# A gate row in four pieces of two column groups, second parts on VectorE, and pooling inputs loaded first, in a hybrid attention, Fourier and pooling layer

## The chip, the cores and the metric

The kernel runs on one core of a Trainium2 chip, as one launch. The metric is the device time of that launch in microseconds. The five engines of the core work from queues of their own, in order, and wait for each other by semaphores: PE is TensorE (matmuls, with their weight loads shown as PEld), DVE is VectorE, ACT is ScalarE, POOL is GpSimd, and SP is SyncE, which here issues all DMA transfers. SBUF is the on-chip memory, PSUM the eight banks into which matmuls accumulate, DRAM the memory outside.

## What is computed

One layer of a diffusion backbone, for 1024 sample tokens and 128 prompt tokens (1152 columns in all), with 1024 channels. The parts of the reference that matter here:

```python
h = _rmsnorm(x, norm_g) * (1 + scale) + shift          # shift, scale, gate = silu(cond) @ w_ada + b_ada
q, k, v, z_a, u_b, z_b, u_c, z_c, g_a, g_b, g_c = jnp.split(h @ w_in, SPLIT_POINTS, axis=-1)
y_a = attend(q, k, v)
y_b = _fourier(u_b, w_fnet)                            # real part of a 2-D DFT, then a linear map
y_c = _pool(u_c, w_pool, pool_scale)                   # windows 2, 4, 8, 16: mean minus self, then a linear map
merged = (sigmoid(g_a) * ((silu(z_a) * y_a) @ p_a)
        + sigmoid(g_b) * ((silu(z_b) * y_b) @ p_b)
        + sigmoid(g_c) * ((silu(z_c) * y_c) @ p_c))
return x + gate * (merged @ w_o), k, v
```

The residual gate is one row of 1024 numbers for each of the two conditionings (context and sample): `silu(cond)` times the last third of `w_ada`, plus its bias. Matmuls are made exact enough by splitting each operand into a high part and a remainder (first part and second part below) and adding three products.

## The kernel before

The program has these stages, one after the other: conditioning and h, the projections with attention (to 427 us), the pooling and Fourier branches (427 to 505 us), the branch projections `p_c`, `p_b`, `p_a` (505 to 636 us), the merge gates (to 884 us), and the output projection.

**Pooling and Fourier branches.** Here the order on each engine is set by the framework's scheduler, which starts from the order of the code. The gates z_c and z_b come in four row tiles of three chunks of 384 columns, 24 matmuls a chunk (`z_chunk`, tiles `zc`, `zb`); after each chunk ACT takes the sigmoid (line 992) and DVE multiplies (line 993). The same call prepares the weights of the next row tile: a matmul sums squares (`pw_m`), DVE, POOL and DVE again make a power of two from it (lines 94, 95, 96, 90; tile `wsc_m`), ACT makes the first part of the weights (line 112, `wh_m`), DVE the second (line 113, `wl_m`). The inputs of the branches, `u`, lie in DRAM and are loaded as `uc` (pooling, two tiles of 128 channels) and `ub` (Fourier, two tiles). For each pooling tile DVE adds shifted copies (`pool_sums`, tiles `s`) and takes the difference from u (`pool_diff`, line 1080); ACT rounds it (`dh`, line 1081), DVE makes the remainder (`dl`, line 1082). Three chunks of three matmuls follow (`pool_out`, tile `yc`), whose results ACT takes out of PSUM (line 1091); `yc` has two PSUM banks, so that the third chunk waits until the first is out. `gate_chunk` multiplies with z, rounds on ACT (line 998, `th`) and makes the second part on POOL (line 999, `tl`). The small tiles of the pooling and channel constants are `pwt`, `ped`, `wpb` and `cw`; `W` is the product of the last.

**Branch projections.** From here the order is written out by hand. `p_chunk(n, c)` is chunk c (384 columns) of row tile n: for n from 0 to 15, 6 matmuls, alternately for p_c (tile `ppc`) and p_b (`ppb`); for n from 16 to 23, 12 matmuls of p_a (`ppa`). There are two PSUM banks for each of the three chunks. ACT copies a chunk to SBUF (line 1278, `pec`, `peb`, six tiles), SP stores it to DRAM (line 1264). DVE splits the weights of row tile n+2 (lines 72 and 73, `oh_p`, `ol_p`) from a raw tile `or` that was loaded four row tiles earlier. Between the chunks of n below 12 stands the gating of branch a: SP loads `ya` and `za` for n+2 (lines 1365 and 1366), ACT takes the sigmoid of `za` (line 1374), DVE multiplies, ACT rounds, POOL makes the second part (line 1383); DVE and ACT also work on combinations of h (`combos`).

**The gate row** is spread over the same 16 row tiles: `add_wg(m)` multiplies the 32 columns of `sil` with one of eight weight tiles `wg` of 128 rows and 1024 columns (two buffers, line 1348 loads them), one matmul for each half of the row (tile `gr`, line 1355), in the group of 32 array columns that m picks (`tile_position`). It is called after row tiles 1, 3, 5 and so on to 15. The four groups of array columns are summed at the end (ACT copies `gro`, matmul `gb`, line 1417). The conditioning stage computes shift and scale in the same way (line 398, tile `pa`), two weight rows of neighbouring column groups at a time.

Of the kernel before, what the change touches and what calls it, by code (L numbers as in the profile page):

```python
# [20 lines left out]
P = 128  # L21
# [18 lines left out]
def mixer_layer(ctx: ExitStack, tc: tile.TileContext, xs, xp, smalls, qgrow, kgrow, bgate, wss, wgate, w1, w3, pw, wo,  # L40
# [154 lines left out]
    with tc.tile_pool(name="hp", bufs=1, side="right") as hp:  # L195
# [770 lines left out]
        with ExitStack() as bctx:  # L966
# [28 lines left out]
            def gate_chunk(zs, y, dh, dl, a):  # L995

                V.tensor_tensor(zs, zs, y[:, a], op=ALU.mult)
                S.copy(dh[:, a], zs)
                G.tensor_tensor(dl[:, a], zs, dh[:, a].bitcast(F32), op=ALU.subtract)

            t_tiles(bctx.enter_context(tc.tile_pool(name="tc", bufs=1, side="right", **TW)), (2, 3))
            with ExitStack() as cctx:
# [23 lines left out]

                pwt = bp.tile([P, 2], F32, name="pwt")
# [13 lines left out]
                us = []  # L1041
                for i, name in enumerate(("c0", "c1", "b0", "b1")):
                    u = bo.tile([P, UW], F32, tag="u", name=f"u{name}", bufs=4)
                    if i < 2:
                        G.memset(u[:, 0:8], 0.0)
                        G.memset(u[:, 1032:1048], 0.0)
                        G.memset(u[:, 1176:1184], 0.0)
                    nc.sync.dma_start(u[:, 8:1032], u_d[i][:, 0:NS])
                    nc.sync.dma_start(u[:, UOFF[1]:UOFF[1] + P], u_d[i][:, NS:NT])
                    us.append(u)  # L1050
                wph, wpl = two(bp, wpb, [P, 2, P], "wp", "wpb")

                def pool_sums(i):
# [6 lines left out]
                    if i == 0:  # L1060
                        e.tensor_copy(s4[0:64, 8:UW - 8], s2[0:64, 8:UW - 8])
# [6 lines left out]
                    e.tensor_copy(s16[0:64, 8:UW - 8], s8[0:64, 8:UW - 8])  # L1068
# [52 lines left out]

                zc1 = new_zs("c1")
# [5 lines left out]
                pool_out(1, *pool_diff(1, f1), zc1)  # L1128
# [60 lines left out]
                zbs = [new_zs("b0"), new_zs("b1")]  # L1189
                zq = []  # L1190

                def next_z():
                    i, c = divmod(len(zq), 3)
                    z_chunk(zbs[i], 10 + i, f"zb{i}", c)
                    zq.append(0)

                yb = [bo.tile([P, UW], F32, tag="u", name=f"yb{i}", bufs=4) for i in range(2)]
                f_ = fold("oe")
                next_z()
# [42 lines left out]
                for c in range(3):  # L1242
                    for i in range(2):
                        a = slice(c * CH, (c + 1) * CH)
                        gate_chunk(zbs[i][:, a], yb[i], th[i], tl[i], a)
# [96 lines left out]
            with tc.tile_pool(name="gp", bufs=1, **TW) as gp:  # L1342
# [9 lines left out]
                def add_wg(m):  # L1352
                    g = 32 * (m % 4)
                    for n in range(2):
# [39 lines left out]
                for n in range(16):  # L1394
# [12 lines left out]
                    if n % 2 == 1:  # L1407
                        add_wg(n // 2)
                        if n // 2 + 2 < 8:
                            load_wg(n // 2 + 2)  # L1410
# [361 lines left out]
```

## Time and profile before

| | us |
|---|---|
| median of three runs | 989.02 (987.64 to 989.61) |
| the profiled execution | 992.83 |
| its span, first to last instruction | 990.3 |
| branches, first zc matmul to first ppc matmul | 426.81 to 504.96 |
| projections p_c and p_b, first ppc matmul to the end of gb | 504.96 to 584.27 |

The profiled execution took 3.8 us longer than the median of the runs; times inside the trace are those of the profiled execution, in microseconds from the start of its span. A row of the timeline gives the start, the duration, the engine, the line, the operation, output and input tiles, and in square brackets how long the engine stood idle before it and what released it. A row of the windows gives a stretch and its length, then busy time (and the number of instructions) of PE, PEld, DVE, ACT and POOL, the granted clock of TensorE (1.00 is full speed), the busy share of the 16 DMA engines and their rate in GB/s.

### The profile page before, as it was taken

How to read it: one execution, taken by the hardware profiler on the slowest of the kernel's cores; microseconds unless marked ns; L12 is line 12 of the kernel's file. 1: busy time of each engine (PE TensorE's matmuls, PEld its weight loads, DVE VectorE, ACT ScalarE, POOL GpSimd, SP SyncE). 2: the span in 40 equal slices, each digit the busy share in tenths (PEclk: the TensorE clock that was granted, in tenths of full speed). 3: DMA queues.
4: the chain of work that ended last, by engine and by line, in shares of the span. 5: the costliest groups of instructions: out<-in, count | busy, mean ns of one | idle time of the engine just before them, and what ended most of it. 6: DMA issues, size and time to landing. Idle time of an engine off the chain costs nothing.

```text
span 990.3 us, 17726 instructions
## 1 busy us (share of the span) xinstructions
PE 922.5 (93%) x6554; PEld 677.0 (68%) x6554; DVE 658.8 (67%) x1443; ACT 489.7 (49%) x1017; POOL 208.4 (21%) x352
## 2 busy tenths in 40 slices
PE   4668899999989999998969999999999999999998
PEld 2324566666656666764757779988888888877886
DVE  2347767767767555549767868478989789765322
ACT  3354757757756646644535644545555454442100
POOL 0000765255254332002132200002021020200000
PEclk9568999999999999998988999999999999999999
DMA  7731351251241141250138965453444332228321
GB/s 300 276 107 37 79 152 44 59 170 34 57 131 33 48 149 55 104 188 0 59 104 291 318 237 197 152 176 96 152 126 122 129 105 79 67 71 297 117 75 53
DMA packets 75781, 125.02 MB, mean 126 GB/s; under 512 B 12031, under 2 KB 45227, under 8 KB 75695
## 3 DMA queue, kind: packets, MB, share of 16 engines
q1 hardware_dynamic: 75695, 123.89, 38.8%
q8 instruction: 51, 0.84, 0.3%
q14 instruction: 35, 0.29, 0.1%
HBM read 88.20 MB, written 29.11 MB: 118 GB/s over the span
## 4 chain that ended last, share of the span: by engine, by line
PE 77%; DVE 7%; ACT 5%; DMA 5%; issue 3%; POOL 2%; SPq 1%; ACTq 0%; DVEq 0%; POOLq 0%
PE p L166 3%; PE p L164 3%; PE p L165 3%; PE wo L164 3%; PE wo L166 3%; PE wo L165 3%; PE xc L164 3%; PE xb L164 3%; PE xb L166 3%; PE xc L166 3%; PE xb L165 3%; PE xc L165 3%; PE m L164 3%; PE m L166 3%; PE m L165 3%; PE xa L164 3%
## 5 line engine op out<-in xcount | busy, mean ns | idle before, releaser
L164 PE MATMUL p<-wh_q,hh 128*128 128x384 f16 x288 | 95.3, 331 | 1.9 <-ACT hh L457 1.9
L166 PE MATMUL p<-wh_q,hl 128*128 128x384 f16 x288 | 95.1, 330 | 1.1 <-DVE hl L458 1.1
L165 PE MATMUL p<-wl_q,hh 128*128 128x384 f16 x288 | 95.1, 330 | 0.0
L733 DVE CUSTOM_DVE_ANT_0 sn<-s,bias 128x512 f32<-128x512 f32 x64 | 44.0, 688 | 32.3 <-PE s L729 30.5
L164 PE MATMUL m<-hh,wh_m 128*128 128x384 f16 x192 | 62.6, 326 | 0.0
L166 PE MATMUL m<-hh,wl_m 128*128 128x384 f16 x192 | 62.6, 326 | 0.0
L165 PE MATMUL m<-hl,wh_m 128*128 128x384 f16 x192 | 62.6, 326 | 0.0
L164 PE MATMUL wo<-woh,mh 128*128 128x512 f32 x144 | 56.8, 394 | 1.2 <-ACT woh L1525 1.2
L165 PE MATMUL wo<-wol,mh 128*128 128x512 f32 x144 | 56.6, 393 | 0.0
L166 PE MATMUL wo<-woh,ml 128*128 128x512 f32 x144 | 56.4, 392 | 0.0
L754 ACT CAST pts<-pt 128x512 f16<-128x512 f32 (+1 forms) x72 | 39.7, 552 | 29.4 <-PE pt L752 28.0
L95 POOL TENSOR_SCALAR wsc_g<-wsc_g 128x1 f32<-128x1 f32 x12 | 2.6, 218 | 222.8 <-DVE wsc_g L94 222.8
L758 DVE TENSOR_TENSOR pts<-pt,pts 128x512 f16<-128x512 f32 (+1 forms) x72 | 46.2, 642 | 3.9 <-ACT pts L754 3.2
L744 ACT ACTIVATE sn<-sn,mn 128x512 f32<-128x512 f32 x64 | 46.2, 721 | 3.9 <-DVE mn L733 3.9
L1654 DVE TENSOR_TENSOR yo<-wo,gb 128x512 f32<-128x512 f32 x18 | 12.4, 691 | 50.1 <-PE wo L166 45.9
L777 DVE TENSOR_SCALAR yt<-po,ri,vf 128x64 f32<-128x64 f32 x72 | 24.7, 343 | 29.7 <-PE po L773 26.4
L166 PEld LDWEIGHTS <-hl 128*128 128x128 f16 x288 | 28.5, 99 | 21.0 <-DVE hl L458 1.8
L164 PEld LDWEIGHTS <-hh 128*128 128x128 f16 x288 | 28.8, 100 | 19.0 <-ACT hh L457 2.0
L166 PEld LDWEIGHTS <-wl_m 128*128 128x128 f16 x288 | 28.4, 99 | 19.3 <-issue 1.3
L164 PEld LDWEIGHTS <-wh_m 128*128 128x128 f16 x288 | 29.0, 101 | 17.3 <-issue 1.1
L290 POOL TENSOR_TENSOR rs<-rs,mhalf 128x4 f32<-128x4 f32 x36 | 40.0, 1110 | 3.0
L165 PEld LDWEIGHTS <-wh_m 128*128 128x128 f16 x288 | 28.4, 99 | 17.3 <-issue 1.0
(650 smaller groups left out, 2950.3 us busy)
## 6 DMA issues: line engine op xcount, KB each, us to landing
wa<-in_wss_dram SPq DMA_DIRECT2D x16, 512.0 KB, 6.3
wr_q<-in_w_dram SPq DMA_DIRECT2D x16, 384.0 KB, 4.9
wr_m<-in_w_dram SPq DMA_DIRECT2D x24, 256.0 KB, 3.1
pp_c<-pec SPq DMA_DIRECT2D x24, 192.0 KB, 6.0
pp_b<-peb SPq DMA_DIRECT2D x24, 192.0 KB, 4.9
pp_a<-pea SPq DMA_DIRECT2D x24, 192.0 KB, 1.8
ppxc<-pp_c SPq DMA_DIRECT2D x16, 288.0 KB, 3.9
ppxb<-pp_b SPq DMA_DIRECT2D x16, 288.0 KB, 3.1
```

The lines of the kernel that those rows point to most:

```text
L95: G.tensor_scalar(sc_[:, 2:3], sc_[:, 2:3], 1e-36, None, op0=ALU.max)
L164: T.matmul(out, lh, rh, start=first, stop=False)
L165: T.matmul(out, lh, rl, start=False, stop=False)
L166: T.matmul(out, ll, rh, start=False, stop=last)
L290: G.tensor_tensor(rs, rs, mhalf, op=ALU.pow)
L733: V.tensor_tensor_reduce(out=sn, in0=pS, in1=bt.rearrange("p a b -> p (a b)"), op0=ALU.add, op1=ALU.min, scale=1.0, scalar=3e38, accum_out=mn)
L744: S.activation(e[:, :n], it["sn"], AF.Exp, bias=it["mn"], scale=-1.0, accum_out=sm_)
L754: S.copy(pts[:, 0, :n], pt[:, :n])
L758: V.tensor_tensor(pts[:, 1, :n], it["pt"][:, :n], pts[:, 0, :n], op=ALU.subtract)
L777: V.tensor_scalar(yt[:, hd * 64:hd * 64 + 64], po[:, :64], ri, c["un"], op0=ALU.mult, op1=ALU.mult)
L1654: V.tensor_tensor(yo, pt, gb[0 if t == 8 else 1][:, cols], op=ALU.mult)
```

## The change

1. `u_load` is a function now. The two pooling tiles of u are loaded before `pwt`, `ped`, `wpb` and `cw` in the code, the two Fourier tiles where all four stood; the six small memsets go from POOL to DVE.
2. In `pool_sums` the plain copy of 64 partitions goes from DVE to ACT, for both tiles.
3. `next_z` (the next chunk of z_b) is called before the matmuls of the second pooling tile, and no longer between the first fold and the first channel transform of the Fourier branch. Of the two z_b tiles the second is made only when it is needed.
4. `gate_chunk` for z_b makes its six second parts on DVE.
5. `add_wg` takes two weight tiles, and for each half of the row multiplies both, in neighbouring column groups. It is called after row tiles 5, 8, 11 and 14; the next two weight tiles are loaded right behind.

```diff
-            def gate_chunk(zs, y, dh, dl, a):
+            def gate_chunk(zs, y, dh, dl, a, eng=G):
                 V.tensor_tensor(zs, zs, y[:, a], op=ALU.mult)
                 S.copy(dh[:, a], zs)
-                G.tensor_tensor(dl[:, a], zs, dh[:, a].bitcast(F32), op=ALU.subtract)
+                eng.tensor_tensor(dl[:, a], zs, dh[:, a].bitcast(F32), op=ALU.subtract)
...
+                us = []
+                def u_load(i, name):
+                    u = bo.tile([P, UW], F32, tag="u", name=f"u{name}", bufs=4)
+                    if i < 2:
+                        V.memset(u[:, 0:8], 0.0)
+                        V.memset(u[:, 1032:1048], 0.0)
+                        V.memset(u[:, 1176:1184], 0.0)
+                    nc.sync.dma_start(u[:, 8:1032], u_d[i][:, 0:NS])
+                    nc.sync.dma_start(u[:, UOFF[1]:UOFF[1] + P], u_d[i][:, NS:NT])
+                    us.append(u)
+                u_load(0, "c0")
+                u_load(1, "c1")
                 pwt = bp.tile([P, 2], F32, name="pwt")
...
                 nc.sync.dma_start(wf, wfnet.rearrange("(a p) j -> p a j", p=P))
-                us = []
-                for i, name in enumerate(("c0", "c1", "b0", "b1")):
...
+                u_load(2, "b0")
+                u_load(3, "b1")
...
-                        e.tensor_copy(s4[0:64, 8:UW - 8], s2[0:64, 8:UW - 8])
+                        S.copy(s4[0:64, 8:UW - 8], s2[0:64, 8:UW - 8])
...
-                    e.tensor_copy(s16[0:64, 8:UW - 8], s8[0:64, 8:UW - 8])
+                    S.copy(s16[0:64, 8:UW - 8], s8[0:64, 8:UW - 8])
...
+                def next_z():
+                    i, c = divmod(len(zq), 3)
+                    if c == 0:
+                        zbs[i] = new_zs(f"b{i}")
+                    z_chunk(zbs[i], 10 + i, f"zb{i}", c)
+                    zq.append(0)
...
-                pool_out(1, *pool_diff(1, f1), zc1)
+                d1 = pool_diff(1, f1)
+                next_z()
+                pool_out(1, *d1, zc1)
...
                 f_ = fold("oe")
-                next_z()
                 a_ = over_channels("oe", *f_)
...
-                        gate_chunk(zbs[i][:, a], yb[i], th[i], tl[i], a)
+                        gate_chunk(zbs[i][:, a], yb[i], th[i], tl[i], a, V)
...
-                def add_wg(m):
-                    g = 32 * (m % 4)
-                    for n in range(2):
+                def add_wg(ms):
+                    for n, m in [(n, m) for n in range(2) for m in ms]:
+                        g = 32 * (m % 4)
                         T.matmul(gbank[n][g:g + 32], sil[:, m], wgs[m][:, n * 512:(n + 1) * 512], start=(m < 4), stop=(m >= 4),
                                  tile_position=(0, g))
...
-                    if n % 2 == 1:
-                        add_wg(n // 2)
-                        if n // 2 + 2 < 8:
-                            load_wg(n // 2 + 2)
+                    if n in (5, 8, 11, 14):
+                        m = 2 * (n // 3 - 1)
+                        add_wg((m, m + 1))
+                        for m in (m + 2, m + 3):
+                            if m < 8:
+                                load_wg(m)
```

What it does to the order on the engines is seen at three places. The numbers behind the names are the program's own and differ between the two programs, and so do line numbers (line 999 is the same; 1355 becomes 1364, 1058 becomes 1064).

On SP, at the start of the pooling branch, before:

```order
L1028 DMA pwt<-in_poolw_dram 128x2
L1030 DMA ped<-in_pooledge_dram 128x32
L1035 DMA wpb<-in_wpool_dram 64x64 x4
L1038 DMA cw<-in_dftch_dram 128x256
L1040 DMA cw<-in_wfnet_dram 128x2x256
L1048 DMA uc_6145<-u_d 128x1024
L1049 DMA uc_6145<-u_d 128x128
L1048 DMA uc_6151<-u_d 128x1024
L1049 DMA uc_6151<-u_d 128x128
L1048 DMA ub_6157<-u_d 128x1024
```

and now:

```order
L1042 DMA pwt<-in_poolw_dram 128x2
L1044 DMA ped<-in_pooledge_dram 128x32
L1035 DMA uc_6132<-u_d 128x1024
L1036 DMA uc_6132<-u_d 128x128
L1035 DMA uc_6138<-u_d 128x1024
L1036 DMA uc_6138<-u_d 128x128
L1049 DMA wpb<-in_wpool_dram 64x64 x4
L1052 DMA cw<-in_dftch_dram 128x256
L1054 DMA cw<-in_wfnet_dram 128x2x256
L1035 DMA ub_6157<-u_d 128x1024
```

The four transfers of the pooling inputs have moved ahead of six transfers of constants, though not ahead of `pwt` and `ped`.

On DVE, at the end of the Fourier branch and the start of the projections (`zsb` is gated z_b, `oh_p` and `ol_p` are split weights of p), before:

```order
L73 TENSOR_TENSOR ol_p_7003<-or_6115,oh_p_7002 128x256
L997 TENSOR_TENSOR zsb_6503<-zsb_6503,yb_6505 128x384
L72 CAST oh_p_7006<-or_6117 128x256
L73 TENSOR_TENSOR ol_p_7007<-or_6117,oh_p_7006 128x256
L997 TENSOR_TENSOR zsb_6504<-zsb_6504,yb_6506 128x384
L72 CAST oh_p_7040<-or_7010 128x256
L73 TENSOR_TENSOR ol_p_7041<-or_7010,oh_p_7040 128x256
```

and now:

```order
L73 TENSOR_TENSOR ol_p_7007<-or_6117,oh_p_7006 128x256
L997 TENSOR_TENSOR zsb_6762<-zsb_6762,yb_6546 128x384
L999 TENSOR_TENSOR tl_6950<-zsb_6474,th_6949 128x384
L999 TENSOR_TENSOR tl_6952<-zsb_6762,th_6951 128x384
L999 TENSOR_TENSOR tl_6950<-zsb_6474,th_6949 128x384
L999 TENSOR_TENSOR tl_6952<-zsb_6762,th_6951 128x384
L999 TENSOR_TENSOR tl_6950<-zsb_6474,th_6949 128x384
L999 TENSOR_TENSOR tl_6952<-zsb_6762,th_6951 128x384
L72 CAST oh_p_7040<-or_7010 128x256
L73 TENSOR_TENSOR ol_p_7041<-or_7010,oh_p_7040 128x256
```

The six subtractions stand between the last product of z_b and the split of the third weight tile.

On PE, the first call of `add_wg`, before (behind row tile 1):

```order
L166 MATMUL ppc_2_7115<-th_6124,ol_p_7007 128x384
L1355 MATMUL gr_7000<-wg_7026,sil 32x512
L1355 MATMUL gr_7001<-wg_7026,sil 32x512
L164 MATMUL ppb_0_7136<-th_6949,oh_p_7040 128x384
L165 MATMUL ppb_0_7136<-tl_6950,oh_p_7040 128x384
```

and now (behind row tile 5):

```order
L1364 MATMUL gr_7000<-wg_7026,sil 32x512
L1364 MATMUL gr_7000<-wg_7028,sil 32x512
L1364 MATMUL gr_7001<-wg_7026,sil 32x512
L1364 MATMUL gr_7001<-wg_7028,sil 32x512
```

Two weight tiles are used at once, and the call stands four row tiles later. The PE order has moved in the pooling branch, too: the first matmul `yc` of the second pooling tile stands behind five matmuls of z_b's second chunk, where it stood behind fourteen, and the third chunk of the first tile behind one matmul of the last zc chunk, where it stood behind five. In both programs the whole first chunk of z_b already stands ahead of the second tile's `yc`.

More of the change, by code (lines that the diff above doesn't have):

```diff
@@ L1040, in mixer_layer @@
                 nc.sync.dma_start(wf, wfnet.rearrange("(a p) j -> p a j", p=P))
-                us = []
-                for i, name in enumerate(("c0", "c1", "b0", "b1")):
[L1043 to L1050, printed above, removed]
+                u_load(2, "b0")
+                u_load(3, "b1")
                 wph, wpl = two(bp, wpb, [P, 2, P], "wp", "wpb")
@@ L1120, in mixer_layer @@
                     V.tensor_tensor(upl[:, ct], u[:, UOFF[1]:UOFF[1] + P], uph[:, ct].bitcast(F32), op=ALU.subtract)
+                zbs = {}
+                zq = []
+                def next_z():
[4 more added lines that the diff above has]
+                    zq.append(0)
                 zc1 = new_zs("c1")
@@ L1187, in keep @@
                     return qs
[L1189 to L1195, printed above, removed]
                 yb = [bo.tile([P, UW], F32, tag="u", name=f"yb{i}", bufs=4) for i in range(2)]
                 f_ = fold("oe")
-                next_z()
                 a_ = over_channels("oe", *f_)
```

## The prediction

> **What bounds the kernel now.** I read the chain of waits first, then PE's windows over the two stretches that the diff touches, then PE's timeline at each hole in them.
>
> ```profile
> span 990.3 us, 17726 instructions
> PE 77%; DVE 7%; ACT 5%; DMA 5%; issue 3%; POOL 2%; SPq 1%; ACTq 0%; DVEq 0%; POOLq 0%
> 504.96:584.27 79.31, 70.56 (x325) 53.52 (x325) 59.50 (x114) 42.62 (x97) 20.65 (x18) 0.94 0.83 272
> 448.00:461.00 13.00, 8.56 (x36) 4.88 (x35) 12.33 (x23) 4.93 (x11) 4.57 (x5) 0.74 0.00 0
> ```
>
> PE carries 77% of the chain, so only time in which PE stands or runs at a low granted clock can be won, or PE work taken away. In the projections of p_c and p_b PE lacks 79.31 - 70.56 = 8.75 us, in the pooling branch 13.00 - 8.56 = 4.44 us, both with a mean clock under 1. Each is one hole:
>
> ```profile
> 454.79 0.69 PE L164 MATMUL yc<-dh,wph 128*128 128x384 f32 x1 [4.44 <-ACT yc L1091]
> 520.34 3.59 PE L1355 MATMUL gr<-wg,sil 128*32 128x512 f32 x4 [8.75 <-DMA wg<-in_wgate_dram]
> 456.00:458.00 2.00, 2.00 (x8) 0.97 (x8) 1.90 (x4) 1.80 (x4) 0.79 (x1) 0.50 0.00 0
> 515.00:520.00 5.00, 0.00 (x0) 0.00 (x0) 4.76 (x10) 3.20 (x9) 1.16 (x1) 0.50 0.92 311
> ```
>
> Behind each the clock is at 0.50 for a while. The prediction has one term for each stretch.
>
> **Pooling branch (change 1, 2, 3).** The third chunk of the first tile waits until ACT has taken the first one out. ACT came late, and the reason reaches back through DVE to the load of u:
>
> ```profile
> 430.30 2.46 SPq L1035 DMA_DIRECT2D wpb<-in_wpool_dram  x4
> 433.91 0.47 SPq L1048 DMA_DIRECT2D uc<-u_d  x1
> 435.56 0.62 DVE L993 SCALAR_TENSOR_TENSOR zsc<-zc,wsc_m,zsc 128x384 f32<-128x384 f32 x1 [0.32 <-ACT zsc L992]
> 439.82 1.39 DVE L1058 TENSOR_TENSOR s<-uc 128x1183 f32<-128x1183 f32 x1 [3.64 <-DMA uc<-u_d]
> 441.25 0.76 DVE L1061 COPY s<-s 64x1168 f32<-64x1168 f32 x1
> 452.28 0.15 DVE L90 TENSOR_SCALAR wsc_m<-wsc_m 128x1 int32<-128x1 int32 x1 [0.54 <-POOL wsc_m L96]
> 452.47 1.34 ACT L112 ACTIVATE wh_m<-wr_m,wsc_m 128x512 f16<-128x512 f32 x2 [1.90 <-DVE s L1057]
> 454.17 1.04 ACT L1091 ACTIVATE yc<-yc,col 128x384 f32<-128x384 f32 x2
> ```
>
> The first u is issued 433.91 - 430.30 = 3.6 us earlier, in the place of wpb, so the first sum starts where the product before it ends, at 436.2 (435.56 + 0.62) instead of 439.82: 3.6. The copy of 64 partitions leaves DVE: 0.76, of which I count 0.4, since its input comes from the sum just ahead and ACT must give it back. DVE is busy 12.33 of 13.00 us afterwards, so the 4.0 reach L90, then the weights on ACT, then the sigmoid and the eviction behind them: PE resumes at 450.8 instead of 454.79. PE comes to that point 0.8 us sooner: only one matmul of the zc chunk stands ahead instead of five, four of 0.163. So the hole is 4.44 - 4.0 + 0.65 = 1.1 to 1.2. With a short hole the clock stays at 1.00, which is worth this:
>
> ```profile
> 457.54 0.52 PE L165 MATMUL zc<-hl,wh_m 128*128 128x384 f16 x1
> 461.14 0.33 PE L164 MATMUL zb<-hh,wh_m 128*128 128x384 f16 x1
> 474.67 0.39 PE L164 MATMUL st1oe<-Wh,foeh 128*128 128x256 f32 x1 [0.62 <-ACT foeh L1023]
> ```
>
> 454.79 to 461.14 took 6.35 us; at full clock the 22 matmuls there take 3.7 (0.163 each, and 0.1 for the change of type), so 2.6 more, with 0.6 us of waiting in all to spare: PE is 6 us ahead at 461.14 after 4.0 + 2.6 - 0.6. That no clock is lost is a choice: a wait of 0.62 us (last row) left it alone, 4.44 did not, and mine lies nearer the first.
>
> What is late next is the second tile, whose matmuls stand behind five z_b matmuls and no longer fourteen:
>
> ```profile
> 466.34 1.24 ACT L1081 CAST dh<-s 128x1024 fp32r<-128x1024 f32 x2 [0.52 <-DVE s L1080]
> 467.44 0.44 PE L164 MATMUL yc<-dh,wph 128*128 128x384 f32 x1
> 461.00:472.00 11.00, 10.89 (x65) 6.52 (x64) 9.71 (x22) 5.49 (x10) 2.29 (x4) 1.00 0.01 2
> ```
>
> Its rounding moves with DVE by 4.0 and a second copy of 0.76, to about 5 us earlier; PE gets there 6 + 1.5 (nine matmuls of 0.163) earlier and waits some 2.3 us. DVE, busy 9.71 of 11.00, holds the gain at 4 through the rest of the branch. **Gain 4.** Its bounds: all holes and the low clock gone give 4.44 + 2.6 + 0.6 = 7.6; PE's waits moving on through a loaded DVE give 0.
>
> What is spent there: cw comes some 1.8 us later behind four issues of u (0.47 each); its product `W` is made by PE at 438.65, a wait of at most 1 that lies before the hole. The six memsets on DVE have no row of their own; by the smallest DVE row above (0.15) they take 0.9 at most, and stand in DVE's wait for the first u. The copies on ACT (about 1.2 by L1081, 0.76 by the row on DVE) fall ahead of 452.47, where ACT had stood 1.90.
>
> The Trainium skill (TensorE: Matmul & The Clock Gate, Part 1: The HAM clock gate) puts the halving at one idle window of about 3.4 us, which runs freely. The holes of 4.44 and 8.75 agree; by it neither 1.2 nor 2.3 would cost clock, and a rate set by the last 0.62 would make the gain 2.6 less.
>
> **Projections (change 4, 5).** The first call of `add_wg` stopped PE, because weight tiles came late:
>
> ```profile
> 511.25 0.34 PE L166 MATMUL ppc<-th,ol_p 128*128 128x384 f32 x1
> 513.04 0.90 SPq L1348 DMA_DIRECT2D wg<-in_wgate_dram  x2
> SPq L1365 <- POOL tl L999: 5.7, 1, 5.7
> 505.52 6.83 POOL L999 TENSOR_TENSOR tl<-zsb,th 128x384 fp32r<-128x384 f32 x6 [29.08 <-ACT th L998]
> 584.20 0.44 PE L164 MATMUL ppa<-ath,oh_p 128*128 128x384 f32 x1
> 530.95 1.90 PE L1355 MATMUL gr<-wg,sil 128*32 128x512 f32 x4
> 38.68 1.89 PE L398 MATMUL pa<-wa,sil 128*32 128x512 f32 x8
> 532.85:539.20 6.35, 6.35 (x37) 6.23 (x36) 5.56 (x12) 4.25 (x10) 2.49 (x2) 1.00 0.88 265
> ```
>
> The call now stands behind row tile 5, where the weights have long landed. And a pair of tiles costs what one did: 1.90 for four records, but 1.89 for eight where the conditioning stage multiplies in neighbouring column groups. So eight calls of 2.0 become four: 8. PE's work alone would be 288 matmuls of 0.172 (6.35 / 37) = 49.6, four calls 8.0, gb 1.9 and 1.3 for ACT's `gro` copies (now behind the last chunk): 61 instead of 79.3. That is 18 (8.75, 8, and 2 for the low clock, less 1.3), if nothing else waits.
>
> Two things do. First, the start: ACT is in order and stands 3.87 and 0.72 us for the first two `za`, which are issued behind the second parts; PE without its hole runs into the evictions queued there. ACT's second sigmoid ends at 518.0 (below); PE then still has three row tiles (9.5, twice 18 matmuls being the 6.35 above), the call (2.0) and two evictions of a sigmoid's length (0.5 each) until the end of the first call, at 530.5. Without the wait it would be there at 511.42 + four row tiles (12.4) + 2.0 = 525.8. So 4.7 are lost and 13.4 left:
>
> ```profile
> 514.12 0.52 ACT L1374 ACTIVATE sga<-za 128x384 f32<-128x384 f32 x1 [3.87 <-DMA za<-za_d]
> 517.47 0.52 ACT L1374 ACTIVATE sga<-za 128x384 f32<-128x384 f32 x1 [0.72 <-DMA za<-za_d]
> 511.25:584.30 73.05, 64.30 (x291) 47.42 (x290) 53.28 (x108) 39.59 (x89) 14.93 (x13) 0.93 0.89 292
> DMA packets 13835, 21.33 MB, mean 292 GB/s; under 512 B 1538, under 2 KB 12034, under 8 KB 13828
> 555.00:560.00 5.00, 5.00 (x23) 3.28 (x22) 3.69 (x10) 2.51 (x6) 1.12 (x1) 1.00 1.02 366
> ACT pec L1278 <- DMA pp_c<-pec: 5.9, 5, 1.9
> ```
>
> Second, the DMA. It is busy for 0.89 x 73.05 = 65.0 us with 21.33 MB: 3.05 us for each MB, none of which the change takes away. ACT already waits 5.9 us for stores of its chunks. PE can be ahead of the stores by twelve chunks of 192 KB (six banks, six tiles), 2.4 MB, and of the last raw weights by 1.05 MB; the other 17.9 MB must have moved when PE is through: 54.6 us of full DMA. With the transfers starting at 512, 1.8 us of slack until 515, and a share of 0.98 behind, that ends at 569.5; with 3.2 for gb the first `ppa` starts at 572.7 instead of 584.20: 11.5. The later limit decides; the pairs of weight tiles, 1 MB at a time, delay stores a little: **gain 11.** Bounds: no run-ahead at all, 512 + 1.8 + 65.0 / 0.98 + 3.2 = 583.3, about 1; no DMA limit, 18.
>
> The Trainium skill (DMA: Bandwidth & Descriptors, Specifications) has a limit of about 358 GB/s for one core. By that, 17.9 MB take an estimated 50.0 us, and the gain would be near 13 by the start limit; the rate of 366 at share 1.02 agrees, the mean of 292 at 0.89 does not.
>
> The six subtractions on DVE have this price:
>
> ```profile
> 505.29 0.55 DVE L997 TENSOR_TENSOR zsb<-zsb,yb 128x384 f32<-128x384 f32 x1
> 505.75 1.11 DVE L72 CAST oh_p<-or 128x256 fp32r<-128x256 f32 x1
> 510.38 1.12 DVE L73 TENSOR_TENSOR ol_p<-or,oh_p 128x256 fp32r<-128x256 f32 x1
> 517.85 0.28 DVE L72 CAST oh_p<-or 128x256 fp32r<-128x256 f32 x1
> ```
>
> 6 x 0.55 = 3.3. But the splits beside POOL's second parts took 1.11 and 1.12, later ones 0.28, so DVE saves some 3 there, and the third split is ready about 511.1, just ahead of PE at 511.25. I take 0; if POOL was not the cause, they cost 3. SP's queued loads behind `tl` go out about 0.9 sooner.
>
> **Sum.** 4 + 11 = 15, worked out in the profiled execution. That took 992.83 as a whole, 3.8 more than the median of 989.02; I take the 15 off the median: **974**.
>
> **Rivals.** B: neither the start nor the DMA limits; 6 + 18 = 24, 965. For it: DMA rates of 366. Against: share 0.92 while PE stood. C: DMA takes most of the second gain, because run-ahead is not used (PE's banks are filled in turn, and an early eviction waits for an early store): 4 + 3 = 7, 982, from 978 to 987. For it: the 5.9 us of waiting, the share of 0.89. D: the pooling part does nothing, since the first z_b chunk stood ahead of the second tile before, and DVE sets the branch: 0 + 11, 978. E, slower: pairs of weight tiles come late. Each is issued behind a call and needed three row tiles, 9.5 us, later. The first took 520.34 - 513.04 = 7.3 us under load. Where a landing exceeds 15 us, each of three calls waits over 5.8 and, with low clock after, up to 8.75 + 2.2 are lost; three make 32.9 against at most 24: 998.
>
> **Numbers.** Forecast 0.53, B 0.12, C 0.22, D 0.07, E 0.06. The likeliest case alone is 970 to 978. The range 964 to 983 leaves out E, the lower part of B (0.05) and the upper of C (0.05). Within 0.2% (2 us, about what can be told from no change) lies only C's far edge: 0.04. Slower: E with a little of C, 0.06; faster 0.90.
>
> **What would show it.** The first `s` near 436; a wait of about 1.2 before the third `yc` at a clock of 1.00 and one of about 2.3 before the second tile; no wait of `gr` for `wg`; four groups of eight `gr` records of about 1.9; ACT waiting for stores of `pec` and `peb` with the DMA share near 1.0 from 515 to 565; the first `ppa` about 15 us earlier, near 569. Wrong would be: `gr` waiting for `wg` again (E), PE's clock at 0.50 around 450, eight records that take 3.8, or PE slack in the projections with a free DMA, when some in-order queue I have not seen sets the pace.

## The result

The changed kernel is faster, by less than half of what was predicted: 982.41 us (979.02 to 984.26) against 989.16 us, a ratio of 0.9936 with the 95% interval 0.9915 to 0.9957. The gain is 6.75 us where 15 was forecast; 982 lies near the upper end of the range (964 to 983), and on the value of rival C. One execution of the kernel with the second parts alone took 2401.2 us and is left out of its median below.

The profiled execution of the changed kernel took 982.22 us, its span 980.4. Its page has these lines for the span and the chain of waits, and the windows view has the projections as a whole:

```profile
span 980.4 us, 17726 instructions
PE 74%; DMA 8%; DVE 7%; ACT 5%; issue 3%; POOL 1%; SPq 1%; ACTq 0%; DVEq 0%; POOLq 0%
500.19:573.91 73.72, 65.51 (x325) 52.31 (x325) 58.39 (x120) 40.67 (x97) 13.29 (x12) 0.98 0.88 291
```

PE lost 3 points of the chain and the DMA won 3. The projections, from the first `ppc` to the first `ppa`, take 73.72 us instead of 79.24, but PE still stands for 8.2 of them (8.75 in the kernel before). The branch stage, from the first `zc` at 425.31 to the first `ppc`, takes 74.88 instead of 78.15. All later stages are equal to within 0.5 us, and 1.5 us of the difference of the spans lie ahead of the first edited line (`zc` at 425.31 and 426.81); in all the executions below that start varies from 423.1 to 428.5, whatever the kernel. So stage lengths are compared below, and medians for the whole.

PE's timeline of the changed kernel, at the places that the prediction named:

```profile
449.13 0.45 PE L164 MATMUL yc<-dh,wph 128*128 128x384 f32 x1 [0.93 <-ACT yc L1097]
460.45 0.76 PE L164 MATMUL yc<-dh,wph 128*128 128x384 f32 x2 [1.92 <-ACT dh L1087]
522.10 0.41 PE L164 MATMUL ppc<-th,oh_p 128*128 128x384 f32 x1 [1.68 <-DVE oh_p L72]
525.52 1.91 PE L1364 MATMUL gr<-wg,sil 128*32 128x512 f32 x8
539.28 4.18 PE L1364 MATMUL gr<-wg,sil 128*32 128x512 f32 x8 [2.28 <-DMA wg<-in_wgate_dram]
553.13 2.32 PE L1364 MATMUL gr<-wg,sil 128*32 128x512 f32 x8
565.11 2.56 PE L1364 MATMUL gr<-wg,sil 128*32 128x512 f32 x8
572.10 1.88 PE L1428 MATMUL gb<-gro,pick 128*2 128x512 f32 x4 [1.10 <-ACT gro L1426]
573.91 0.44 PE L164 MATMUL ppa<-ath,oh_p 128*128 128x384 f32 x1
```

The holes of 4.44 and 8.75 us are gone, eight records take 1.91 us where four took 1.90, and the two smaller waits of the pooling branch are there (0.93 and 1.92). New is a wait of 2.28 us of the second call, whose eight records then take 4.18. After the first call the stretch has no hole as large as the old one, and yet the forecast end is missed. The lines of the other engines, and the DMA's total until the first `ppa`:

```profile
434.60 1.39 DVE L1064 TENSOR_TENSOR s<-uc 128x1183 f32<-128x1183 f32 x1
502.11 2.90 DVE L999 TENSOR_TENSOR tl<-zsb,th 128x384 fp32r<-128x384 f32 x6
504.92 0.29 DVE L72 CAST oh_p<-or 128x256 fp32r<-128x256 f32 x1
504.56 0.33 SPq L1374 DMA_DIRECT2D ya<-yT_d  x1
ACT pec L1287 <- DMA pp_c<-pec: 8.9, 3, 4.3
566.71 0.48 ACT L1287 COPY pec<-ppc 128x384 f32<-128x384 f32 x1 [4.29 <-DMA pp_c<-pec]
571.08 0.48 ACT L1287 COPY peb<-ppb 128x384 f32<-128x384 f32 x1
571.45 1.08 ACT L1426 COPY gro<-gr 128x512 f32<-128x512 f32 x2
DMA packets 13740, 21.20 MB, mean 306 GB/s; under 512 B 1523, under 2 KB 11940, under 8 KB 13734
```

The last line covers 504.56 to 573.91: 21.20 MB have moved before the first `ppa`, nearly all of the 21.33 MB that moved in the stretch before. ACT's evictions of p_c chunks wait 8.9 us for stores (5.9 before), 4.29 at once near the end, and the copies of the gate row follow its last eviction.

### The profile page after: what moved, and what is told of

Its sections match the earlier page's. It is cut to its first block, busy times and chain, and to the rows that moved or that the text cites. A ratio compares the mean times of both kernels' runs of the same rounds, so it can differ in the third digit from the quotient of the medians.

```text
span 980.4 us, 17726 instructions
## 1 busy us (share of the span) xinstructions
PE 918.3 (94%) x6554; PEld 677.2 (69%) x6554; DVE 656.3 (67%) x1453; ACT 488.8 (50%) x1019; POOL 202.4 (21%) x340
## 4 chain that ended last, share of the span: by engine, by line
PE 74%; DMA 8%; DVE 7%; ACT 5%; issue 3%; POOL 1%; SPq 1%; ACTq 0%; DVEq 0%; POOLq 0%
PE p L166 3%; PE p L164 3%; PE p L165 3%; PE wo L164 3%; PE wo L166 3%; PE wo L165 3%; PE m L164 3%; PE m L166 3%; PE m L165 3%; PE xc L164 3%; PE xb L164 3%; PE xb L166 3%; PE xb L165 3%; PE xc L165 3%; PE xc L166 3%; PE xa L164 3%
## 5 line engine op out<-in xcount | busy, mean ns | idle before, releaser
L164 PEld LDWEIGHTS <-hh 128*128 128x128 f16 x288 | 28.8, 100 | 19.0 <-ACT hh L457 2.0
L164 PEld LDWEIGHTS <-wh_m 128*128 128x128 f16 x288 | 28.9, 100 | 17.2 <-issue 0.6
L165 PEld LDWEIGHTS <-hh 128*128 128x128 f16 x288 | 28.5, 99 | 17.1 <-issue 0.8
```

The costliest lines, as they stand in the source:

```text
L164: T.matmul(out, lh, rh, start=first, stop=False)
L165: T.matmul(out, lh, rl, start=False, stop=False)
```

## The experiments

Two theories were put against each other after the result. **D** (not the prediction's rival D): the DMA's bytes set the end of the projections, so that PE work taken away there only turns into other waits. **W** (and, later, **P**): PE's own work and its waits for late weight tiles set it, above all the 2.28 us wait and the halved clock behind it. Other runs undo one part of the change or do one alone. Each ratio is against the kernel before on the same chip, whose median was between 988.17 and 989.47 in these comparisons; it was taken from the runs of both and is not the quotient of two medians of the table. Medians of two rows can come from different chips, so gains in us are worked out from the ratios, at 989 us, unless a median is named. Stage lengths come from one profiled execution each, and those of one kernel differ by up to 2.4 us.

| kernel | median us | ratio, 95% interval | branch | projections | p_a |
|---|---|---|---|---|---|
| before (read for the prediction) | 989.02 | 1 | 78.15 | 79.24 | 51.64 |
| before, profiled again | 988.94 (one) | | 76.74 | 78.00 | 51.64 |
| changed | 982.41 | 0.9936, 0.9915 to 0.9957 | 74.88 | 73.72 | 51.61 |
| changed, again | 984.69 | 0.9948, 0.9930 to 0.9967 | 75.14 | 75.62 | 51.64 |
| pooling edits alone (1 to 3) | 986.21 | 0.9974, 0.9956 to 0.9993 | 73.86 | 77.48 | 51.64 |
| second parts on VectorE alone (4) | 986.49 | 0.9975, 0.9955 to 0.9995 | 77.34 | 75.46 | 51.64 |
| gate row alone (5) | 986.60 | 0.9980, 0.9967 to 0.9994 | 76.44 | 75.91 | 51.63 |
| changed, row as before (1 to 4) | 985.59 | 0.9966, 0.9953 to 0.9979 | 75.17 | 75.46 | 51.64 |
| changed, second parts on POOL | 987.32 | 0.9978, 0.9966 to 0.9990 | 74.90 | 77.12 | 51.64 |
| changed, z_b chunk in its old place | 983.02 | 0.9928, 0.9914 to 0.9943 | 75.31 | 74.08 | 51.64 |
| early pairs | 982.71 | 0.9937, 0.9911 to 0.9962 | 73.95 | 71.27 | 51.63 |
| early pairs, profiled again | 980.76 (one) | | 74.81 | 73.64 | 51.64 |
| two weight tiles loaded | 976.22 | 0.9876, 0.9854 to 0.9898 | 75.30 | 67.60 | 51.62 |
| two calls of four | 984.47 | 0.9968, 0.9952 to 0.9984 | 74.83 | 75.13 | 52.45 |
| no loads of ya | 977.65 | 0.9899, 0.9876 to 0.9923 | 74.90 | 73.48 | 51.62 |
| two pairs in p_a | 980.61 | 0.9906, 0.9889 to 0.9922 | 75.08 | 64.90 | 57.67 |
| the same, gating later | 979.76 | 0.9909, 0.9888 to 0.9931 | 73.92 | 65.23 | 58.19 |
| all pairs in p_a | 988.42 | 1.0005, 0.9991 to 1.0020 | 74.91 | 62.86 | 69.40 |

### The changed kernel once more

> The changed kernel once more, for a second profiled execution and for the comparison on one chip: time 981 to 984. If the 2.28 us wait of the second call is a steady part of it, it is seen again at 1.5 to 3 us with the halved clock behind it; if it belongs to one execution, the lost time shows in other waits (stores, za) with the stretch at 72 to 75 all the same.

984.69, 2.3 us above the first median and 0.7 above what was expected. A call waits for its pair again, for 0.90 and then 1.43 us at 540 to 543, and ACT waits 10.0 us for stores of `pec`; the stretch is 75.62. So both kinds of wait came again, in other sizes.

### Early pairs

```diff
-wgs[m] = gp.tile([P, D], F32, tag="wg", name=f"wg{m}", bufs=2)
+wgs[m] = gp.tile([P, D], F32, tag="wg", name=f"wg{m}", bufs=4)
...
-    for m in (m + 2, m + 3):          # behind the calls of n = 5, 8, 11
+if n in (2, 5, 8):                    # one call earlier
+    for m in (2 * (n // 3) + 2, 2 * (n // 3) + 3):
```

> Four weight buffers: the pairs of weight tiles are loaded one call earlier than in the changed kernel (the bias row is loaded late and the sigmoid has one buffer, to make room). Theory W (the pair for the second call came too late, PE stood 2.28 us and the clock was then halved): no call waits, the stretch from the first ppc to the first ppa falls from 73.7 us to 68.5 to 70, the time from 982.4 to 977 to 979. Rival D (the DMA is full in this stretch, and the wait only moves to the stores): stretch 72.5 to 74, time 981 to 983, ACT waits some 4 us longer for stores of its chunks.

PE's calls in the profiled execution:

```profile
523.97 1.91 PE L1363 MATMUL gr<-wg,sil 128*32 128x512 f32 x8
536.08 1.91 PE L1363 MATMUL gr<-wg,sil 128*32 128x512 f32 x8
549.22 1.91 PE L1363 MATMUL gr<-wg,sil 128*32 128x512 f32 x8
561.56 1.91 PE L1363 MATMUL gr<-wg,sil 128*32 128x512 f32 x8
```

No call waits any more and all four take 1.91. The median is 982.71 all the same, that of the changed kernel. The late pair was real, and taking it away was worth nothing that can be measured: the 3.4 to 5.4 us that W expected are not there, though the interval (0.9911 to 0.9962) leaves room for some 2 us. To make room for the buffers, this kernel also has one tile for the sigmoid of `za` instead of two; whether that takes back a part of a gain was not tried apart. The stretch in this execution was short (71.27, in the range of neither theory); the execution itself was 4.7 us faster than the median.

> The kernel with early pairs once more, one look: its median was that of the changed kernel, though its first profiled execution was 4.7 us faster than that median. Theory D: in an execution near the median no call waits for weight tiles, but ACT waits for its stores, and the stretch is 73 to 76. Rival P: a call waits for its pair again.

In the second profiled execution of this kernel, too, no call waits, and the stretch is 73.64, as long as in the changed kernel. PE stands 9.5 us of it (8.2 in the changed kernel), now for evictions and for split weights. ACT, which makes the evictions, waits 9.7 us for `za` and 7.2 for its stores. That D's longer waits for stores would take the place of the late pair did not show: they were 12.7 us in the changed kernel.

### Two weight tiles, two calls, no ya

```diff
-        for m in (m + 2, m + 3):
-            if m < 8:
-                load_wg(m)
+        wgs[m + 2], wgs[m + 3] = wgs[m], wgs[m + 1]     # six loads fewer
```

> The changed kernel without six of the eight loads of gate weights (the first two tiles are used four times, so the gate row is not the reference's): 3 MB less for the DMA. Theory W: no call waits, stretch 67 to 69.5, time 976 to 978.5. Rival D: 9 us of DMA time fall away and PE's own 67 us decide: stretch about 67, time about 976. Together with the run with early pairs: if that one is as slow as the changed kernel and this one is fast, D holds; if both are fast, W.

976.22, 6.2 us less than the changed kernel, with a stretch of 67.60, as both theories had it. By itself this does not tell bytes from waits; together with the early pairs it does, since those remove the waits for pairs and keep the bytes. The next run keeps the bytes, too, and takes PE work away:

```diff
-                        add_wg((m, m + 1))
+                        if m < 4:
+                            add_wg((m, m + 1))
```

> The changed kernel with two of the four gate-row calls left out (the last 8 of 16 column-group products; the row is not the reference's), all eight loads kept: 3.8 us less PE work, the same bytes. Theory D (the DMA sets the end of the stretch from the first ppc to the first ppa): stretch 72.5 to 75.5 as now, time 981.5 to 984. Rival P (PE's work and its waits for late weight tiles set it): 68 to 71, time 977 to 979.5.

```profile
501.58:576.71 75.13, 63.00 (x308) 51.25 (x309) 58.41 (x120) 40.62 (x97) 13.55 (x12) 0.94 0.87 287
567.71 0.48 ACT L1287 COPY pec<-ppc 128x384 f32<-128x384 f32 x1 [4.52 <-DMA pp_c<-pec]
568.24 0.69 PE L164 MATMUL ppb<-th,oh_p 128*128 128x384 f32 x1 [2.13 <-ACT pec L1287]
572.55 1.08 ACT L1427 COPY gro<-gr 128x512 f32<-128x512 f32 x2
573.21 3.58 PE L1429 MATMUL gb<-gro,pick 128*2 128x512 f32 x4 [2.68 <-ACT gro L1427]
```

PE is busy 63.00 us instead of 65.51, and the stretch is no shorter: 75.13. PE now stands 2.13 us for an eviction that waited 4.52 us for a store, and 2.68 for `gro`, behind which the four records of `gb` take 3.58 instead of 1.88. The median is 984.47, the ratio 0.9968 where the changed kernel had 0.9936 and 0.9948. This is the clearest of the runs: two calls of 1.91 us less in this stretch, and nothing gained. P falls.

```diff
-                    nc.sync.dma_start(y, yT_d[i][:, a])
...
-                        V.tensor_tensor(z, z, y, op=ALU.mult)
+                        V.tensor_tensor(z, z, sg, op=ALU.mult)
```

> The changed kernel without the loads of ya (2.4 MB less; branch a is gated with sigmoid times za times sigmoid, so the output is not the reference's), the same PE work, the same gate-weight loads. Theory D: 2.4 MB at 2 to 3 us each, stretch 67.5 to 70, time 975.5 to 978.5. Rival P: PE still waits for weight tiles and works as long, stretch 71.5 to 74, time 980 to 983.

The median, 977.65, is where D put it; by the ratio (0.9899) that is 3.7 or 4.9 us better than the changed kernel in its two comparisons. The one profiled execution does not fit: it took 979.77, and its stretch 73.48, in P's range and not in D's 67.5 to 70. Its DMA share was 0.80 (0.65 from 516 to 522), and yet ACT waited 8.7 us for stores of `pec`; why, is open. So bytes taken away bring 1.5 to 2.3 us for each MB by the ratios (5.9 or 7.1 us for 3.1 MB, 3.7 or 4.9 for 2.4), but that the DMA is *always* full in this stretch is not shown.

### One part alone, one part undone

The gate row, taken out of the changed kernel and put alone into the one before:

```diff
-                    if n in (5, 8, 11, 14):
-                        m = 2 * (n // 3 - 1)
-                        add_wg((m, m + 1))
+                    if n % 2 == 1:
+                        add_wg(n // 2)
```

> The changed kernel with the gate row as before (eight calls of one tile). The parts add up: the pooling branch keeps its 3.8 us, the hole before the first gate matmul is back at 8 to 9 us, stretch 78 to 79.5, time 985 to 986, slower than the changed kernel by 3 to 5.5. Rival (the second parts on VectorE let the loads go out early and shorten that hole by themselves): stretch 75 to 77, time 983 to 984.

985.59, slower than the changed kernel by about 3, as the sum of parts had it; but the stretch is 75.46 and not 78 to 79.5, in the rival's range, and the hole before the first gate matmul 5.23 and not 8 to 9.

> The kernel before with the gate row in four pieces alone. The parts add up: branch stage 78 us as before, stretch 73.5 to 75, time 983.5 to 986. Rival (the row needs the second parts on VectorE, since POOL's hold back the first loads by 1 us and slow the splits): stretch 75.5 to 78, time 986 to 988.5.

986.60, a gain of 2.0; time and stretch (75.91) are in the rival's range. That the row needs the second parts for more is not shown by that: with them there it is worth 1.7 or 2.9 us (5.1 or 6.3 of the whole change less 3.4 of the kernel without it).

The second parts, back on POOL in the changed kernel, and on VectorE alone in the one before:

```diff
-                        gate_chunk(zbs[i][:, a], yb[i], th[i], tl[i], a, V)
+                        gate_chunk(zbs[i][:, a], yb[i], th[i], tl[i], a)
```

> The changed kernel with the second parts of z_b on POOL again. If they matter: the first loads of the projections go out about 1 us later and the splits beside POOL take 1.1 us instead of 0.28, the stretch from the first ppc to the first ppa grows by 0.5 to 2.5, time 983 to 985. Rival (the DMA decides the stretch and PE's start is slack): 981.5 to 983.

> The kernel before with the second parts of z_b on VectorE alone. Theory S (the DMA of the projections starts when the second parts end, 1.9 us earlier so, and the stretch hangs on the DMA): 1.5 to 3 us gained, time 986 to 987.5. Rival (the gain of this part shows only with the other parts): 988.5 to 989.5.

987.32 and 986.49: undone they cost more than expected (4.2 or 3.0 us against the changed kernel by the ratio; the time is above both ranges), alone they bring 2.5, as the theory of the earlier start had it.

The three edits of the pooling branch alone (the row and the second parts as before), and the changed kernel with the z_b chunk in its old place:

```diff
-                d1 = pool_diff(1, f1)
-                next_z()
-                pool_out(1, *d1, zc1)
+                pool_out(1, *pool_diff(1, f1), zc1)
...
                 f_ = fold("oe")
+                next_z()
```

> The kernel before with the three edits of the pooling branch alone. If the branch keeps what its profile shows (75.1 us against 76.4 to 78.2 of the kernels with the old branch): 1.5 to 3 us gained, time 986 to 987.5. Rival (given back in the projections, where PE waits for the DMA anyway): 988.5 to 989.5.

> The changed kernel with the chunk of z_b called in its old place. Theory V (VectorE sets the branch stage; PE's wait of 1.92 us before the second pooling tile and the halved clock behind it are slack): branch stage 74 to 75 us as in the changed kernel, time 981.5 to 983. Rival (the earlier call brought part of the 3.8 us): branch stage 76 to 78, time 984 to 986.

986.21, a gain of 2.6, kept to the end. The other run does not test what it was made for. The call stands in its old place in the code, but PE's rows of the whole branch stage come in the same order as in the changed kernel, with the same five z_b matmuls and the same wait of 1.92 us ahead of the second pooling tile: the scheduler undid the move. So what the place of the chunk is worth stays open, and the run is a third one of the changed kernel's order: 983.02, branch 75.31, projections 74.08. There the second call waits only 0.83 us for its pair (2.28 and 2.33 in the other two, with stretches of 73.72 and 75.62), which is one more sign that this wait does not set the length.

Alone, the three parts are worth nearly the same: pooling 2.6 us (0.0026 of 989), second parts 2.5, the row 2.0. They sum to 7.1, and all together gave 6.3 and 5.1. Undone one by one they are less regular: without VectorE's second parts the gain is only 2.2, less than the row and the pooling edits gave apart (4.6). With intervals of 2.4 to 4 us in width I read no more into that than that the second parts carry a good share.

The profile of the kernel with the second parts alone shows how they act:

```profile
513.20 3.30 PE L1355 MATMUL gr<-wg,sil 128*32 128x512 f32 x4 [5.93 <-DMA wg<-in_wgate_dram]
505.02 0.33 SPq L1365 DMA_DIRECT2D ya<-yT_d  x1
500.65 0.44 PE L164 MATMUL ppc<-th,oh_p 128*128 128x384 f32 x1 [0.24 <-DVE oh_p L72]
```

SP's first load goes out 4.37 us after the first `ppc` (505.02 - 500.65), as in the changed kernel (504.56 - 500.19), where it was 6.29 (511.25 - 504.96) behind POOL. The whole train of transfers starts 1.9 us earlier, and the hole ahead of the first gate matmul falls to 5.93.

From the issue of that first load to the first `ppa` the time is much the same in all kernels that move these bytes: 69.35, 71.25 and 69.71 us in the three executions of the changed kernel's order, 70.76 with two calls, 69.63 with the row alone, 70.83 with the second parts on POOL, 71.08, 71.09 and 71.21 in the three kernels with pieces of the change but the old row, 72.95 and 71.71 in the kernel before. Only the early pairs lie below (66.43 and 68.80). So an earlier start of the loads moves the end by as much, and the new row takes one or two us off the way.

### The kernel before, once more

> The kernel before once more, for a second profiled execution. If the profiled execution that the prediction read was a slow one in its two holes: the hole at the third yc is 2 to 4 us instead of 4.44, the one before the first gate matmul 5 to 7.5 instead of 8.75, and the stretch 75.5 to 78.5 instead of 79.2. Rival (it was typical): all three within 0.5 of those values.

```profile
437.03 1.39 DVE L1058 TENSOR_TENSOR s<-uc 128x1183 f32<-128x1183 f32 x1 [2.25 <-DMA uc<-u_d]
452.00 0.45 PE L164 MATMUL yc<-dh,wph 128*128 128x384 f32 x1 [3.05 <-ACT yc L1091]
515.99 3.59 PE L1355 MATMUL gr<-wg,sil 128*32 128x512 f32 x4 [7.22 <-ACT pec L1278]
```

The wait for u was 2.25 us here and not 3.64, the hole at the third `yc` 3.05 and not 4.44, the one at the gate matmul 7.22 and not 8.75. The execution that the prediction read was the longer one at both places; its branch and projections were together 2.65 us longer than here. Its branch, 78.15, is the longest of the four with the old order (76.44, 76.74 and 77.34 in the others).

### A version that uses the finding

If bytes set the projections, gate weights should be loaded where the DMA has room. In the p_a stage it does:

```diff
-                    if n in (5, 8, 11, 14):
+                    if n == 5:            # pair 0, then loads of pair 1
...
+                    if n == 11:           # pair 1
...
+                        if (m, c) == (1, 2):      # in p_a, row tile 17: pair 2, loads of pair 3
+                        if (m, c) == (3, 2):      # row tile 19: pair 3, copies gro
+                        if (m, c) == (4, 1):      # gb, g_d
```

> The changed kernel with the last two of the four gate-row calls, their 2 MB of loads and the sum of the row in the p_a stage (pairs behind row tiles 5, 11, 17 and 19). Theory D (the p_c and p_b stretch is bound by the DMA): that stretch falls from 73.7 to 63.5 to 66 (5.1 us of PE work and 6.4 us of DMA go), p_a takes 57 to 58 instead of 51.6, time 977 to 979.5. Rival (p_a cannot take the loads beside its stores, or something else sets the first stretch): the two sum to 124 to 126 as now, time 981 to 983.5.

```profile
505.90:566.40 60.50, 54.29 (x282) 47.47 (x281) 51.10 (x104) 34.17 (x81) 13.22 (x12) 0.97 0.88 285
566.40:624.00 57.60, 56.51 (x312) 50.91 (x310) 37.17 (x84) 29.00 (x64) 0.79 (x2) 1.00 0.61 213
```

The projections fall to 64.90 and p_a takes 57.67, both as D had it, with PE busy 56.51 of 57.60 us at a DMA share of 0.61. The time, 980.61, is 1.1 us above D's range and below the rival's. PE work moves here along with the bytes, so this run alone does not tell one from the other. On the same chip, in the same comparison, the changed kernel took 984.69 (0.9930 to 0.9967) and this one 980.61 (0.9889 to 0.9922): the intervals do not meet. This kernel and the next, which cannot be told from it, are the fastest here of those that leave nothing out:

> As the kernel with the last two pairs in p_a, and the gating of branch a begins two row tiles later (row tiles 2 to 14 instead of 0 to 12), so that ACT's first sigmoid does not stand in front of the evictions while za is on its way. Theory (the start of the stretch is lost to that in-order wait, 2.2 us and the half clock behind it): stretch 60.5 to 63.5 instead of 64.9, time 976.5 to 979. Rival (the DMA sets the end of the stretch all the same): 64 to 66, time 980 to 981.5.

```diff
-                        if n < 12:
-                            a_gate(n, c)
+                        if 2 <= n < 14:
+                            a_gate(n - 2, c)
```

(The loads of `ya` and `za` are issued one row tile later, too.) The projections stay at 65.23, as the rival had it: the start waits that this was meant to remove came back in other places (3.11 us for an eviction at 515.53). The time, 979.76, lies between the two theories.

> The changed kernel with all four gate-row calls and all eight loads in the p_a stage (4 MB less in the p_c and p_b stretch). Theory D: that stretch falls to 57 to 61, p_a takes 61 to 63 (four calls, the sum), time 976.5 to 979.5. Rival (start waits and in-order evictions hold the first stretch above 62, or p_a is held up by its own loads, above 65): 980 to 983.

This was no better than the kernel before, which neither side expected. The projections fell further, to 62.86, though not to D's 57 to 61, and the first pair now lands late at the head of p_a:

```profile
570.02 1.04 PE L1363 MATMUL gr<-wg,sil 128*32 128x512 f32 x2 [1.45 <-DMA wg<-in_wgate_dram]
573.41 3.62 PE L1363 MATMUL gr<-wg,sil 128*32 128x512 f32 x6 [2.35 <-DMA wg<-in_wgate_dram]
562.00:575.00 13.00, 9.20 (x44) 6.75 (x43) 9.18 (x22) 4.33 (x10) 0.00 (x0) 0.90 0.95 312
```

p_a grew by 17.8 us, where four calls and the sum are 9.5 (4 x 1.91 + 1.88). Most of the other 8.3 lies here: 3.8 us of waits, 2.75 by which the first call's records (1.04 + 3.62) are longer than 1.91, and a clock of 0.50 from 574 to 578 behind them. The rest was not traced.

## Why the prediction was right or wrong

**Direction and mechanism of the parts: right.** The first `s` starts 9.3 us after the first `zc` instead of 13.0 (3.7 earlier, 3.6 forecast; 2.3 earlier than in the second execution of the kernel before, at 11.6). The waits at the third `yc` and the second tile were 0.93 and 1.92 (1.2 and 2.3 forecast). The call of `gr` costs 1.91 for eight records. The full DMA time of the stretch is 0.88 x 73.72 = 64.9 us (65.0 forecast).

**The step that failed is the run-ahead in the DMA's term of the projections.** The prediction let PE be ahead of the stores by twelve chunks and of the raw weights by 1.05 MB, so that only 17.9 of 21.33 MB had to move before PE was through. When PE's last product of the stretch was done (571.00), 20.23 MB had moved, 20.10 in the second execution:

```profile
DMA packets 13072, 20.23 MB, mean 304 GB/s; under 512 B 1445, under 2 KB 11400, under 8 KB 13066
557.77 6.71 DMA wg<-in_wgate_dram
564.54 5.21 DMA pp_c<-pec
569.86 0.96 ACT peb L1287 x2
571.08 0.48 ACT peb L1287
571.56 0.50 ACT gro L1426
572.10 1.88 PE gb L1428 x4
```

The first line is for 504.56 to 571.00, the others are the end of the chain of waits up to the first `ppa` (start, duration, what). The 2.3 MB more are 7.1 us at 3.05 us for each MB, 7.3 at the share of 0.98. That is more than the miss: the forecast end lay 67.8 us behind the first `ppc`, the measured one 73.72, which is 5.9 more. Against the 7.3, and 1.7 because the DMA ran below the share of 0.98, stand 2.7 of an earlier start (4.37 instead of 7.04 behind the first `ppc`) and 0.3 of a shorter end.

Half of the 7.1 stood in the text itself: it put the `gro` copies behind ACT's last chunk, and counted the six banks (1.2 MB, 3.6 us) that ACT must empty before as run-ahead. The chain shows the order: the last pair of weight tiles, a store behind it, ACT's last evictions, `gro`, and then PE's `gb`. In this execution PE's own last product ended at 571.00, too, so the chain alone does not say how much the stores held it; the run with two calls says it, where PE is through 68.8 us behind the first `ppc` instead of 70.8 and then stands 2.68 us for `gro`. Why the six tiles and the raw weights, the other half, did not help is not shown.

By the prediction's own sum with the start as it was (504.56), all of the run-ahead gives a first `ppa` at 565.3 and none of it 575.9; it came at 573.91. So most of the run-ahead was not there, which is the view of rival C. That the time, too, is C's 982 is in part luck: of its 4 + 3, the pooling branch brought 2.6 and the projections 2.4 to 5.5 by their profiled lengths (the two of the kernel before against the two of the changed one), with 1.9 of that from the earlier start.

**The second parts on VectorE were priced at nothing and are worth 2.5 us alone.** Their cost was sized well (2.90 for six, 3.3 forecast), and POOL was the cause of the slow splits (0.29 beside no POOL work, 1.11 before, and 1.11 again with the second parts back on POOL). What was missed is the consequence of the term that I judged to be decisive: if the DMA sets the end, its start counts in full. The prediction had the first load 0.9 earlier, set it beside the sum, and added nothing; it was 1.9 earlier.

**The pooling branch was mis-sized.** Forecast 4, measured 2.6 alone by the ratio (3.3 between the two profiled executions first compared). Two causes are seen. The holes read were large ones of one execution (3.05 instead of 4.44 in the second). And the choice that no clock is lost failed: behind the wait of 1.92 us the clock fell to half in 11 of 14 executions, and that cost the branch about 1 us (last section).

**Rival E** happened at one call of three, at less than half of its price (2.28 us of waiting and 2.27 of slower records, where it had up to 8.75 + 2.2), and not by its condition: the pair landed in 7.2 us and not in 15. It was issued at 532.00, 4.6 us behind the call that freed its buffers, because SP's queue had loads and stores ahead of it; the prediction took it as issued right behind. Early pairs removed that and brought nothing that can be told. **Rival B** (no limit) is refuted by the stretch of 73.72, and the prediction's rival D (the pooling part brings nothing) by the pooling edits alone (0.9956 to 0.9993).

## What to carry to other kernels

In a stretch where the DMA share is near 0.9 and an engine already waits for its stores, price every edit in bytes and in the start of the transfers first; here fewer instructions on PE turned into other waits, and the same work moved to a stage with a free DMA brought 2 to 4 us more. Count buffers as run-ahead only if nothing that belongs to the stage must wait, in order, until they are emptied. When a framework's scheduler sets the order, see in the trace that an edit changed the order at all before reading its time. And read a second profiled execution before sizing a hole that ends on a transfer: here the two holes differed by 1.4 and 1.5 us between executions of one kernel, together a third of the 8 us that the forecast was off.

## What the runs showed of the hardware

**The clock halves after shorter waits than expected.** In the changed kernel it fell to half behind a wait of 1.92 us, and behind the one of 2.28:

```profile
462.50:464.00 1.50, 1.50 (x7) 1.19 (x6) 1.02 (x2) 0.49 (x1) 0.00 (x0) 0.50 0.00 0
541.00:543.00 2.00, 2.00 (x7) 0.53 (x3) 0.00 (x0) 1.28 (x3) 0.99 (x1) 0.58 0.79 271
```

In its second execution the same wait of 1.92 us, up to 462.54, left the clock up for 2 us and had it at half for the next 2:

```profile
462.60:464.50 1.90, 1.67 (x8) 0.93 (x9) 1.79 (x6) 1.78 (x4) 0.09 (x2) 0.97 0.00 0
464.50:466.50 2.00, 2.00 (x8) 1.35 (x8) 1.79 (x4) 1.16 (x2) 0.00 (x0) 0.50 0.00 0
```

The wait of 1.68 in the first left it alone. The same wait before the second pooling tile stands in 14 of the profiled executions, always 1.92 or 1.93 us long, and in three of them the clock stayed up:

| executions | clock behind the wait | branch stage, us |
|---|---|---|
| 11 | at half for 3.4 us, beginning 0.2 to 1.9 us after the wait | 74.81 to 75.31 |
| 3 (pooling edits alone, early pairs, gating later) | 1.00 | 73.86 to 73.95 |

So the same instructions with the same wait cost about 1 us more or less. Two executions of the kernel with early pairs fell on different sides (73.95 and 74.81). Waits of 2.87, 3.05 and 3.81 us at the third chunk were followed by half clock for 3.4 us, too; waits up to 1 us in this stage never were. The Trainium skill (TensorE: Matmul & The Clock Gate, Part 1: The HAM clock gate) gives a free-running idle window of about 3.4 us; its free-running fits a drop that comes sooner, later or not at all after the same wait, but a wait of 1.92 us is shorter than one window, so the length does not agree with these runs.

**POOL's subtractions beside VectorE slow VectorE's splits** from 0.28 to 1.11 us (`oh_p`) and from 0.42 to 1.12 (`ol_p`); with the subtractions on VectorE all six took 2.90 us, less than half of POOL's 6.83.
